# A fused transformer layer on one core: a rearranged start, a third PSUM bank for the maxima, and five small jobs moved between engines

## The chip, the cores and the metric

The kernel runs on one core of a Trainium2 chip. The metric is device time in microseconds (us) of one execution; lower is better. A core has a matrix engine (TensorE, PE; its weight loads are listed apart as PEld), a vector engine (VectorE, DVE), a scalar engine (ScalarE, ACT), a general engine (GpSimd, POOL), and queues that issue DMA transfers (here SP's and ACT's). PE writes its results into PSUM, which this kernel uses as eight banks of 128 partitions × 512 fp32 elements; all else lies in SBUF.

## The reference

One layer of a diffusion backbone. 128 context tokens (the prompt) and 1024 latent tokens are normalised and modulated, projected once, put through two groups of attention heads in parallel, gated, projected back, and added to the input.

```python
shift, scale, gate = modulation(c, w_mod[l], b_mod[l])          # silu(c) @ w_mod + b_mod
h = rmsnorm(xs, norm_gain[l]) * (1.0 + scale) + shift
q_a, k_a, v_a, g_a, q_b, k_b, v_b, g_b = project(h, w_in[l], ...)   # h @ w_in, RMS norm of q and k per head
...                                                             # rotary positions on q and k of latent tokens
o_a = global_attn_latent(q_a, k_a, v_a, cache_k_a[:, l], cache_v_a[:, l])            # all keys
o_b = window_attn_latent(q_b, k_b, v_b, cache_k_b[:, l], cache_v_b[:, l], sink_b[l])  # |i-j| <= 128, and a sink
xs = xs + gate * merge_out(o_a, g_a, o_b, g_b, w_out[l])        # concat(o_a*silu(g_a), o_b*silu(g_b)) @ w_out
```

The prompt goes through the same with its own modulation and sees only itself. D is 1024; each group has 8 query heads and 2 key heads of 64. Keys, values and the prompt's keys and values are outputs too.

## The kernel before

**Arithmetic.** Where fp32 accuracy is wanted, an operand is split into a high part in the matrix engine's fp32r type and the remainder, also fp32r: `hi` is a cast, `lo = raw - hi` a subtraction. A product is then three matmuls: hi·hi, hi·lo and lo·hi.

**Order.** The instructions of every engine run in the order in which the Python code emits them (`in_order` chains them). A small agenda puts work off: `later(n, f)` runs `f` at the n-th next `tick()`, and in attention one tick is one slot. So moving a line or changing a slot number moves instructions on every engine that it touches.

**The start.** Tokens come in nine tiles of 128 (tile 0 is the prompt, 1 to 8 are latent). `load_x` loads a tile through SP's queue; `squares` (ACT) and two small GpSimd operations give the reciprocal root mean square; `scaled` (DVE) multiplies; `turned_tile` transposes the tile on PE, by a 128×128 identity, into two PSUM tiles px (`px{t}_0` for the first four column blocks, `px{t}_1` for the others); `keep` copies them to `xT`. The identity comes by DMA (L321) and is cast to bf16 as `ident_b`. `modulate_rows(j)` (L353) multiplies the conditioning vectors with channel block j of the modulation weights `wm` (eight row products into one bank, pm, then one copy, mrows); `modulate(j)` transposes that back and reduces it to per-channel factors `a_mod`, `b_col`. `modulated(j, ...)` makes the block's input: ACT writes h's high part, DVE the full value hf, GpSimd the remainder (L410 to L412). `warm(n)` runs n matmuls of the bf16 identity with itself, whose result nobody reads (L431). The first gate product (L270) waits for `modulated(0, 1, 4, 0)`.

**The gates of mixer A.** A loop over channel blocks j = 1 to 8 adds channel block j-1's contribution to the gate columns: `first_gates` for the first 512 tokens, in banks `pg*_f`, and `next_gates` for the next 256 tokens, one block behind, in two banks `pg*_s`. After that come the queries, keys and values, the gates of mixer B, and the splits of the output weights w_out (16 pieces of 128×512; hi by a cast, lo by a subtraction, L1043 and L1044).

**Attention.** From about 298 us on the work runs in slots, one block of 128 keys against 512 queries (4 heads × 128) per slot. In each slot `scores` issues the score products (st, L1170 and L1171) or, for windowed heads, transposes of probabilities (L1165); ACT takes the exponential (pe, L1173) and its high part (ph, L1177), GpSimd or DVE the remainder (pl). Three slots later `values` multiplies with the value blocks (pv, L1191 to L1194). Between them the slot's due items run: row maxima for a later unit (pmx on PE, L889, then a maximum on DVE, L890), windowed scores in natural layout (sn, L944 and L945, DVE's mask and minimum L948, ACT's exponential pen, L934), transposes of small vectors, late pieces of w_out (`WO_LATE` gives the slot at which each is loaded; the split follows three slots later), and output products. At a unit's end, `inverse` (rs, L1203 for windowed heads, L1205 and L1206 for global ones), `gated` and `parts` (ogh, L1227, and its remainder) make the gated output's two parts.

**PSUM.** The eight banks carry letters: A, B, C with two each, D and E with one. In attention A serves pmx, sn and the small transposes in turn, B the scores, C the pv, D and E the two column halves of the output products (po); D also serves the last piece of mixer B's gates during the first slots.

A unit is one latent tile, one key head and one mixer: 9 slots for a global unit, 3 or 4 for a windowed one. Units 0 to 3 are latent tile 1 (24 slots), units 4 to 7 latent tile 2 (26 slots). Units 0 and 2 have their maxima taken before attention starts.

Of the kernel before, what the change touches and what calls it, by code (L numbers as in the profile page):

```python
# [50 lines left out]
WO_LATE = {12: 13, 13: 20, 11: 27, 14: 29, 15: 31}  # L51
# [10 lines left out]
LAST_ORDER = ((0, 0), (0, 1), (1, 0), (1, 1), (2, 0), (2, 1))  # L62
SECOND_FROM = 5
WARM = (8, 4)
# [51 lines left out]
def hybrid_step(ctx, tc, x_prompt, x_sample, cache_k_a, cache_v_a, cache_k_b, cache_v_b,  # L116
                cols, w_mod_ss, w_mod_g, b_mod, w_in, qn_a, kn_a, qn_b, kn_b, sink_b, w_out,
                k_ident, k_cos, k_sin, k_mask,
# [200 lines left out]
    with tc.tile_pool(name="st", bufs=2, side="right") as st:  # L319
        ident = st.tile([P, P], F32, name="ident", bufs=1)  # L320
        nc.sync.dma_start(ident, k_ident)  # L321
# [4 lines left out]
        nc.sync.dma_start(colt, cols)  # L326
# [22 lines left out]
        def modulate_rows(j):  # L349
            pm = pmod[j] = bank_tr(f"pm{j}")  # L350
            for k in range(KT):
                a = 32 * (k % 4)
                nc.tensor.matmul(pm[a : a + 32, 0:256], sil32[:, k, :], wm[j][:, k].rearrange("p s n -> p (s n)"),  # L353
                                 start=(k < 4), stop=(k >= 4), tile_position=(0, a))
            mrows[j] = st.tile([P, 256], F32, tag="mrows", name=f"mrows{j}")
            (nc.scalar.copy if j > 1 else nc.vector.tensor_copy)(mrows[j], pm[:, 0:256])
# [29 lines left out]
        def scaled(t):  # L386
            nc.vector.tensor_scalar(xn[t], xn[t], rx.pop(t), None, op0=ALU.mult)

        def turned_tile(t, tags, between=None):

            for c in range(2):
                if c and between:
                    between()
                px[t, c] = bank(tags[c], f"px{t}_{c}")
                for i in range(4):
                    k = 4 * c + i
                    nc.tensor.transpose(px[t, c][:, P * i : P * i + P], xn[t][:, P * k : P * k + P], ident)
# [5 lines left out]
        def modulated(j, t0, n, cond):  # L403

            w = P * n
            dst = slice(P * place(t0), P * place(t0) + w)
            i, to = third(dst)
            a, b = (x[:, j, cond : cond + 1] for x in (a_mod, b_col))
            hf = st.tile([P, 512], F32, tag="hf", name=f"hf{j}_{t0}", bufs=3)
            nc.scalar.activation(h_at(0, i, j, to), xT[:, j, dst], AF.Identity, scale=a, bias=b)  # L410
            nc.vector.tensor_scalar(hf[:, :w], xT[:, j, dst], a, b, op0=ALU.mult, op1=ALU.add)
            nc.gpsimd.tensor_tensor(h_at(1, i, j, to), hf[:, :w], h_at(0, i, j, to), op=ALU.subtract)  # L412
# [50 lines left out]
        modulated(0, 1, 4, 0)
# [5 lines left out]
        warm(WARM[1])  # L469
# [4 lines left out]
        for j in range(1, KT + 2):  # L474
# [397 lines left out]
    def max_items(i):  # L872
# [4 lines left out]
        def item(h, b):  # L877
# [4 lines left out]
            pm = bank("A", f"pmx{i}_{h}_{b}")  # L882
# [33 lines left out]
    def weight_items(i):  # L916
# [20 lines left out]
        def item(h):  # L937
# [5 lines left out]
            s = bank("A", f"sn{i}_{h}")[:, 0:n]  # L943
# [95 lines left out]
    def split_wo(i):  # L1039
        raw = wo_raw.pop(i)  # L1040
        hi, lo = (wo_place(j, i) for j in range(2))
        wo_parts[i] = hi, lo
        (nc.scalar.copy if i < 7 or i in WO_LATE else nc.vector.tensor_copy)(hi, raw)  # L1043
        (nc.gpsimd if i in WO_LATE or i % 2 else nc.vector).tensor_tensor(lo, raw, hi, op=ALU.subtract)  # L1044

# [111 lines left out]
    def scores(i, b, blk):  # L1157
# [4 lines left out]
        if m == 1:  # L1162
# [3 lines left out]
            nc.scalar.copy(ph, s)  # L1166
# [17 lines left out]
    def values(i, b, last, blk, ph, pl):  # L1184
# [15 lines left out]
        def inverse():  # L1200
            v["rs"] = w2.tile([64, 512], F32, tag="rs", name=f"rs{i}", bufs=1)
            if m == 1:
                nc.scalar.copy(v["rs"], pv[64:128, :])  # L1203
                return
# [16 lines left out]
        def parts():  # L1221
# [5 lines left out]
            nc.scalar.copy(oh, v["of"])  # L1227
# [90 lines left out]
    for s in range(len(slots) + LAG + PROMPT_END[3]):  # L1318
        tick()
# [29 lines left out]
def _consts():  # L1349
# [15 lines left out]
        "k_ident": np.eye(P, dtype=f),  # L1365
# [43 lines left out]
```

## Time and profile before

| | us |
|---|---|
| Time, median of 3 runs | 704.11 (703.66 to 704.31) |
| The profiled execution, its own time | 703.62 |
| Its span, first to last instruction | 701.4 |
| PE busy | 690.6 |
| DVE, ACT, POOL busy | 462.5, 419.2, 337.9 |
| First gate product starts | 16.76 |
| Attention slots start | about 298 |

A row of the timeline reads: start in us, duration in us, engine, line and operation, output <- inputs, partitions × elements and types, and in brackets how long the engine stood before it and on what. Several like instructions in a row are folded to one row with their count. PE's records overlap, so two starts are compared rather than a start with an end. The records name the line of the kernel that ran; in the changed kernel the same code has higher line numbers.

### The profile page before, as it was taken

To read this page: it belongs to the slowest core of one execution; us is meant where nothing else is said; L and a number is where in the kernel's file an instruction comes from. 1 tells how busy PE (TensorE), PEld (TensorE's weight loads), DVE (VectorE), ACT (ScalarE), POOL (GpSimd) and SP (SyncE) were. 2 spreads that over 40 slices of the span, in tenths; PEclk is the share of its full clock that TensorE was granted. 3 is DMA by queue.
4 is the path that set the end of the run, shared out by engine and by line. 5 is a ranking of instruction groups with operands and counts; after the bars stand their busy time and mean duration, and the time that the engine had idled before them with its cause. 6 is when DMAs were issued, how large, how long until landed. Compare 5 with 4: busy or idle time off the path is not lost.

```text
span 701.4 us, 10680 instructions
## 1 busy us (share of the span) xinstructions
PE 690.6 (98%) x3532; PEld 559.5 (80%) x3532; DVE 462.5 (66%) x998; ACT 419.2 (60%) x858; POOL 337.9 (48%) x358
## 2 busy tenths in 40 slices
PE   7999999999999999999999999999999999999997
PEld 4778988878788889986788787788887888887876
DVE  4667257968768854676667567567676775775563
ACT  6646411422313423399877887787788778877870
POOL 3547024233313321267676654765575557455752
PEclk9999999999999999999999999999999999999999
DMA  8962283349344016332222121122221221212324
GB/s 319 412 214 111 78 306 75 91 131 279 87 124 132 16 61 209 129 84 77 75 83 89 47 83 54 62 67 75 69 75 40 68 91 46 82 54 91 92 75 128
DMA packets 53703, 78.57 MB, mean 112 GB/s; under 512 B 7112, under 2 KB 25864, under 8 KB 52752
## 3 DMA queue, kind: packets, MB, share of 16 engines
q1 hardware_dynamic: 45952, 66.74, 28.9%
q10 hardware_dynamic: 7696, 11.15, 5.8%
q8 instruction: 28, 0.46, 0.3%
q14 instruction: 27, 0.22, 0.1%
HBM read 58.69 MB, written 19.18 MB: 111 GB/s over the span
## 4 chain that ended last, share of the span: by engine, by line
PE 94%; ACT 2%; DVE 2%; DMA 1%; issue 0%; POOL 0%; SPq 0%; ACTq 0%; DVEq 0%
PE po L1262 14%; PE pv L1191 7%; PE pv L1194 7%; PE pmx L889 5%; PE st L1170 5%; PE pv L1193 5%; PE pq L256 5%; PE pq L258 5%; PE st L1171 5%; PE pq L257 5%; PE st L1165 4%; PE pg L266 3%; PE pg L270 3%; PE pg L271 3%; PE pk L257 2%; PE pk L258 2%
## 5 line engine op out<-in xcount | busy, mean ns | idle before, releaser
L1181 POOL TENSOR_TENSOR pl<-pe,ph 128x512 fp32r<-128x512 f32 x130 | 167.8, 1293 | 142.7 <-DVE nm L948 64.4
L890 DVE TENSOR_REDUCE mx<-pmx 128x1 f32<-128x384 f32 x192 | 101.3, 552 | 58.5 <-PE pmx L889 56.0
L1173 ACT ACTIVATE pe<-st 128x512 f32<-128x512 f32 x146 | 86.8, 595 | 27.3 <-PE st L1171 26.5
L1177 ACT CAST ph<-pe 128x512 fp32r<-128x512 f32 x146 | 90.7, 621 | 4.8
L1191 PE MATMUL pv<-ph,v_hi 128*128 128x512 f32 x208 | 82.4, 396 | 0.1
L1194 PE MATMUL pv<-pl,v_hi 128*128 128x512 f32 x208 | 81.9, 394 | 0.0
L948 DVE CUSTOM_DVE_ANT_0 sn<-sn,mask,nsink 128x512 f32<-128x512 f32 (+1 forms) x64 | 46.3, 724 | 43.3 <-PE sn L945 39.2
L1262 PE MATMUL po<-wo,ogh 128*128 128x512 f32 (+1 forms) x224 | 73.2, 387 | 0.0
L181 POOL TENSOR_TENSOR rs_q<-ms_q,mhalf 128x8 f32<-128x8 f32 x18 | 34.1, 1896 | 80.9 <-DVE ms_q L179 80.9
L889 PE MATMUL pmx<-kha,qt 128*128 128x384 f32 x192 | 61.6, 365 | 1.1 <-ACT pen L934 0.8
L1170 PE MATMUL st<-qt,kha 128*128 128x512 f32 x144 | 57.7, 401 | 0.1
L1193 PE MATMUL pv<-ph,v_lo 128*64 128x512 f32 x146 | 57.7, 395 | 0.0
L1171 PE MATMUL st<-qb,kla 68*128 68x512 f32 x144 | 57.3, 398 | 0.0
L1194 PEld LDWEIGHTS pv<-pl,v_hi 128*128 128x128 f32 x208 | 39.0, 188 | 16.8
L934 ACT ACTIVATE pen<-sn,nm 128x512 f32<-128x512 f32 (+2 forms) x72 | 45.0, 626 | 5.7 <-DVE nm L948 2.3
L1166 ACT CAST ph<-st 128x512 fp32r<-128x512 f32 x62 | 36.4, 587 | 19.9 <-PE st L1165 19.6
L653 ACT CAST qo0q<-ptq 128x512 fp32r<-128x512 f32 x18 | 10.6, 586 | 60.4 <-PE ptq L650 58.8
L1262 PEld LDWEIGHTS po<-wo,ogh 128*128 128x128 f32 x224 | 41.0, 188 | 6.4
L1191 PEld LDWEIGHTS pv<-ph,v_hi 128*128 128x128 f32 x208 | 39.2, 189 | 7.8 <-issue 0.8
L1167 DVE TENSOR_TENSOR pl<-st,ph 128x512 fp32r<-128x512 f32 x62 | 42.6, 688 | 2.1 <-ACT ph L1166 1.4
L1262 PE MATMUL po<-wo,ogl 128*128 128x512 f32 (+1 forms) x112 | 43.5, 388 | 0.0
L889 PEld LDWEIGHTS pmx<-kha,qt 128*128 128x128 f32 x192 | 35.5, 190 | 7.3 <-DVE mx L890 1.8
(224 smaller groups left out, 1703.5 us busy)
## 6 DMA issues: line engine op xcount, KB each, us to landing
qt<-qd SPq DMA_DIRECT2D x36, 256.0 KB, 2.9
wm<-in_w_mod_ss_dram SPq DMA_DIRECT2D x7, 1024.0 KB, 9.7
qd<-qo0q ACTq DMA_DIRECT2D x36, 128.0 KB, 2.4
sgl<-gd SPq DMA_DIRECT2D x36, 128.0 KB, 2.3
out_dram<-yt SPq DMA_DIRECT2D x17, 256.0 KB, 2.1
xn<-in_x_sample_dram SPq DMA_DIRECT2D x8, 512.0 KB, 6.8
wg<-in_w_mod_g_dram SPq DMA_DIRECT2D x4, 1024.0 KB, 8.5
wraw<-in_w_out_dram SPq DMA_DIRECT2D x16, 256.0 KB, 4.5
```

The lines of the kernel that those rows point to most:

```text
L257: nc.tensor.matmul(out, h_at(0, i, k, tok), w.lo[k], start=False, stop=False)
L889: nc.tensor.matmul(pm[:, 0:384], lhs, kha[:, g, 3 * b : 3 * b + 3, :], start=True, stop=True)
L890: nc.vector.tensor_reduce(mx[:, h, b : b + 1], pm[:, 0:384], axis=AX.X, op=ALU.max)
L1170: nc.tensor.matmul(s, kh, qtile[i], start=True, stop=False)
L1171: nc.tensor.matmul(s, kl, qbtile[i], start=False, stop=True)
L1173: nc.scalar.activation(pe, s, AF.Exp)
L1177: nc.scalar.copy(ph, pe)
L1181: nc.gpsimd.tensor_tensor(pl, pe, ph, op=ALU.subtract)
L1191: nc.tensor.matmul(pv, two, ph, start=(b == 0), stop=False)
L1193: nc.tensor.matmul(pv[0:64, :], vl, ph, start=False, stop=False)
L1194: nc.tensor.matmul(pv, two, pl, start=False, stop=last)
L1262: nc.tensor.matmul(po[c][:, at], a, wo_parts[KT * n + k][lo][:, at], start=(k == KS[0] and p == 0), stop=(k == KS[-1] and p == 2))
```

## The change

- The identity is built on GpSimd (a fill and a select along the diagonal) instead of loaded; `colt`, the small table of columns, is loaded by ACT's queue. SP's first DMA is now x's.
- `modulate_rows(0)`, px3 and px4 are done in halves, with the halves that `modulate(0)` does not need behind it; `scaled(4)` is two instructions. `warm` runs 14 products first, then 2, 2 and 2 between the tiles, and 4 at the end, in place of 8 and 4.
- In `modulated(0, 1, 4, 0)` ACT writes h's first 256 columns and DVE the other 256.
- At j = 8 the small products of the first two column groups (six matmuls of 256 columns) go ahead of `first_gates` for channel block 7.
- pmx, sn and the two small transposes take banks A, A and E in turn until slot 24; after it A alone, as before.
- rs of unit 1 (a copy) goes from ACT to DVE, ogh of unit 0 from ACT to GpSimd. `PHB_DVE` is empty and changes nothing.
- The remainders of w_out 0, 2, 4, 6 go from DVE to GpSimd. The late pieces 12 and 13 are loaded at slots 23 and 24 instead of 13 and 20, pieces 11, 14 and 15 one slot earlier than before.

```diff
-WO_LATE = {12: 13, 13: 20, 11: 27, 14: 29, 15: 31}
+SMALL_FIRST = 2
+LO_POOL = (0, 2, 4, 6)
+WO_LATE = {12: 23, 13: 24, 11: 26, 14: 28, 15: 30}
...
+RS_DVE = (1,)
+PHB_DVE = ()
+OG_POOL = (0,)
+AUX = ((24, "AAE"),)
-WARM = (8, 4)
+WARM = (14, 2, 2, 2, 4)
...
+    aux_tags = ["A"]
+
+    def bank_aux(name):
+        turn["aux"] += 1
+        return bank(aux_tags[0][turn["aux"] % len(aux_tags[0])], name)
...
-        nc.sync.dma_start(ident, k_ident)
+        nc.gpsimd.memset(ident, 0.0)
+        nc.gpsimd.affine_select(ident, ident, pattern=[[-1, P]], compare_op=ALU.not_equal, fill=1.0, base=0,
+                                channel_multiplier=1)
...
-        nc.sync.dma_start(colt, cols)
+        nc.scalar.dma_start(colt, cols)
...
-        def modulate_rows(j):
-            pm = pmod[j] = bank_tr(f"pm{j}")
-            for k in range(KT):
+        def modulate_rows(j, ks=range(KT)):
+            if 0 in ks:
+                pmod[j] = bank_tr(f"pm{j}")
+            pm = pmod[j]
+            for k in ks:
...
+            if KT - 1 not in ks:
+                return
...
-            nc.scalar.activation(h_at(0, i, j, to), xT[:, j, dst], AF.Identity, scale=a, bias=b)
+            own = w // 2 if shared else w
+            nc.scalar.activation(h_at(0, i, j, slice(to.start, to.start + own)), xT[:, j, dst.start : dst.start + own],
+                                 AF.Identity, scale=a, bias=b)
+            if shared:
+                nc.vector.tensor_scalar(h_at(0, i, j, slice(to.start + own, to.stop)), xT[:, j, dst.start + own : dst.stop],
+                                        a, b, op0=ALU.mult, op1=ALU.add)
...
         warm(WARM[0])
-        for t, tags in ((1, "AB"), (2, "AB"), (3, "CC")):
+        for t in (1, 2):
             scaled(t)
-            turned_tile(t, tags)
+            turned_tile(t, "AB")
+            warm(WARM[t])
             if t > 1:
                 for c in range(2):
                     keep(t - 1, c, copies[c])
-        scaled(4)
-        modulate_rows(0)
+        scaled(3)
+        modulate_rows(0, range(4))
+        turned_half(3, 0, "C")
+        warm(WARM[3])
+        for c in range(2):
+            keep(2, c, copies[c])
+        scaled(4, 2)
+        modulate_rows(0, range(4, KT))
         keep(3, 0, copies[0])
         W_GA.split(nc.gpsimd)
-        turned_tile(4, "AB", lambda: modulate(0))
+        turned_half(4, 0, "A")
+        modulate(0)
         keep(4, 0, copies[0])
-        modulated(0, 1, 4, 0)
+        turned_half(3, 1, "C")
+        turned_half(4, 1, "B")
+        modulated(0, 1, 4, 0, True)
...
-        warm(WARM[1])
+        warm(WARM[4])
...
+            if j == KT:
+                for ch in range(SMALL_FIRST):
+                    next_gates(ch, j - 2)
             if big_on:
                 first_gates(0, j - 1, 0)
...
-                if small_on:
+                if small_on and not (j == KT and ch < SMALL_FIRST):
                     next_gates(ch, j - 2)
...
-            pm = bank("A", f"pmx{i}_{h}_{b}")
+            pm = bank_aux(f"pmx{i}_{h}_{b}")
...
-            s = bank("A", f"sn{i}_{h}")[:, 0:n]
+            s = bank_aux(f"sn{i}_{h}")[:, 0:n]
...
-        (nc.gpsimd if i in WO_LATE or i % 2 else nc.vector).tensor_tensor(lo, raw, hi, op=ALU.subtract)
+        (nc.gpsimd if i in WO_LATE or i % 2 or i in LO_POOL else nc.vector).tensor_tensor(lo, raw, hi, op=ALU.subtract)
...
-                nc.scalar.copy(v["rs"], pv[64:128, :])
+                (nc.vector.tensor_copy if i in RS_DVE else nc.scalar.copy)(v["rs"], pv[64:128, :])
...
-            nc.scalar.copy(oh, v["of"])
+            (nc.gpsimd.tensor_copy if i in OG_POOL else nc.scalar.copy)(oh, v["of"])
...
     for s in range(len(slots) + LAG + PROMPT_END[3]):
+        aux_tags[0] = next((tags for until, tags in AUX if s < until), "A")
```

What moves where, at three places. PE's program between the transposes of tile 3 and the first gate product, before (x4 marks four like instructions; xn_181 is tile 3, xn_183 tile 4):

```order
L397 MATMUL px_0_268<-ident,xn_181 128x128 x4
L397 MATMUL px_1_273<-ident,xn_181 128x128 x4
L353 MATMUL pm_281<-wm_185,sil_173 32x256 x8
L397 MATMUL px_0_299<-ident,xn_183 128x128 x4
L362 MATMUL pm_281<-ident,mrows_290 128x128 x2
L397 MATMUL px_1_310<-ident,xn_183 128x128 x4
```

The same stretch now (xn_184 is tile 3, xn_186 tile 4):

```order
L369 MATMUL pm_283<-wm_188,sil_176 32x256 x4
L414 MATMUL px_0_288<-ident,xn_184 128x128 x4
L457 LDWEIGHTS ident_b
L457 MATMUL idle<-ident_b 128x512
L457 LDWEIGHTS ident_b
L457 MATMUL idle<-ident_b 128x512
L369 MATMUL pm_283<-wm_188,sil_176 32x256 x4
L414 MATMUL px_0_313<-ident,xn_186 128x128 x4
L380 MATMUL pm_283<-ident,mrows_304 128x128 x2
L414 MATMUL px_1_325<-ident,xn_184 128x128 x4
L414 MATMUL px_1_330<-ident,xn_186 128x128 x4
```

Both second halves (px_1) now stand behind the transposes of the modulation rows.

PE's program at j = 8, before: the products of h's remainder (h_0_7_130, L266) come as the fifth and sixth step.

```order
L270 MATMUL pg_0_f<-h_0_7_122,whiga_789 128x512
L271 MATMUL pg_0_f<-h_0_7_122,wloga_790 128x512
L270 MATMUL pg_1_f<-h_0_7_122,whiga_789 128x512
L271 MATMUL pg_1_f<-h_0_7_122,wloga_790 128x512
L266 MATMUL pg_0_f<-h_0_7_130,whiga_789 128x512
L266 MATMUL pg_1_f<-h_0_7_130,whiga_789 128x512
```

The same place now:

```order
L282 MATMUL pg_0_s<-h_1_6_134,whiga_738 128x256
L283 MATMUL pg_0_s<-h_1_6_134,wloga_739 128x256
L278 MATMUL pg_0_s<-h_1_6_138,whiga_738 128x256
L282 MATMUL pg_0_s<-h_1_6_134,whiga_738 128x256
L283 MATMUL pg_0_s<-h_1_6_134,wloga_739 128x256
L278 MATMUL pg_0_s<-h_1_6_138,whiga_738 128x256
L282 MATMUL pg_0_f<-h_0_7_122,whiga_809 128x512
L283 MATMUL pg_0_f<-h_0_7_122,wloga_810 128x512
L282 MATMUL pg_1_f<-h_0_7_122,whiga_809 128x512
L283 MATMUL pg_1_f<-h_0_7_122,wloga_810 128x512
L278 MATMUL pg_0_f<-h_0_7_130,whiga_809 128x512
```

Six products of the other 256 tokens stand ahead.

ACT's program in latent tile 1, from the exponential of the third windowed score of unit 1 on, before:

```order
L934 ACTIVATE pen_3609,sum_3611<-sn_2_3651,nm_3610 128x384
L1203 COPY rs_3662<-pv_3618 64x512
L1173 ACTIVATE pe_3_3669<-st_3_3664 128x512
L1177 CAST ph_3_3665<-pe_3_3669 128x512
L1043 CAST wo_big_3683<-wraw_3633 128x512
L934 ACTIVATE pen_3609,sum_3611<-sn_3_3673,nm_3610 128x384
L1173 ACTIVATE pe_4_3693<-st_4_3688 128x512
L1177 CAST ph_4_3689<-pe_4_3693 128x512
L1227 CAST ogh_3703<-spare 128x256
```

Now:

```order
L973 ACTIVATE pen_3629,sum_3631<-sn_2_3669,nm_3630 128x384
L1212 ACTIVATE pe_3_3687<-st_3_3682 128x512
L1216 CAST ph_3_3683<-pe_3_3687 128x512
L973 ACTIVATE pen_3629,sum_3631<-sn_3_3691,nm_3630 128x384
L1212 ACTIVATE pe_4_3707<-st_4_3702 128x512
L1216 CAST ph_4_3703<-pe_4_3707 128x512
```

Between the exponentials stood a copy (rs), a cast of w_out (wo_big) and a cast of the gated output (ogh); all three are gone from ACT here.

More of the change, by code (lines that the diff above doesn't have):

```diff
@@ L117, in hybrid_step @@
                 cols, w_mod_ss, w_mod_g, b_mod, w_in, qn_a, kn_a, qn_b, kn_b, sink_b, w_out,
-                k_ident, k_cos, k_sin, k_mask,
+                k_cos, k_sin, k_mask,
                 y_prompt, y_sample, new_k_a, new_v_a, new_k_b, new_v_b):
@@ L146, in hybrid_step @@
     BANKS = {"A": 2, "B": 2, "C": 2, "D": 1, "E": 1}
-    turn = {"mm": 0, "tr": 0}
+    turn = {"mm": 0, "tr": 0, "aux": 0}
     mm_tags = ["BAAB"]
@@ L384, in squares, with scaled, turned_half, turned_tile @@
             nc.gpsimd.tensor_tensor(rx[t], ms, mhalf[:, 0:1], op=ALU.pow)
-        def scaled(t):
-            nc.vector.tensor_scalar(xn[t], xn[t], rx.pop(t), None, op0=ALU.mult)
-        def turned_tile(t, tags, between=None):
-            for c in range(2):
[L392 to L397, printed above, removed]
+        def scaled(t, parts=1):
+            r = rx.pop(t)
+            for p in range(parts):
+                half = xn[t][:, D // parts * p : D // parts * (p + 1)]
+                nc.vector.tensor_scalar(half, half, r, None, op0=ALU.mult)
+        def turned_half(t, c, tag):
+            px[t, c] = bank(tag, f"px{t}_{c}")
+            for i in range(4):
+                k = 4 * c + i
+                nc.tensor.transpose(px[t, c][:, P * i : P * i + P], xn[t][:, P * k : P * k + P], ident)
+        def turned_tile(t, tags):
+            for c in range(2):
+                turned_half(t, c, tags[c])
         def keep(t, c, copy):
@@ L401, in keep, with modulated @@
             copy(xT[:, 4 * c : 4 * c + 4, at], px.pop((t, c)).rearrange("p (k n) -> p k n", n=P))
-        def modulated(j, t0, n, cond):
+        def modulated(j, t0, n, cond, shared=False):
             w = P * n
@@ L904, in transpose @@
         def transpose():
-            pt = bank("A", f"ptm{i}")
+            pt = bank_aux(f"ptm{i}")
             nc.tensor.transpose(pt[0:4, 0:P].bitcast(F32R), m_nat[i // 2 % 2], ident_r)
@@ L994, in turned @@
         def turned():
-            v["pt"] = bank("A", f"pti{i}")[0:4, 0:P]
+            v["pt"] = bank_aux(f"pti{i}")[0:4, 0:P]
             nc.tensor.transpose(v["pt"], v["inv"], ident_r.bitcast(F32))
@@ L1165, in scores @@
                 nc.tensor.transpose(s[:, P * h : P * h + P], penat[i][:, h, o : o + P], ident_r.bitcast(F32))
-            nc.scalar.copy(ph, s)
+            (nc.vector.tensor_copy if (i, b) in PHB_DVE else nc.scalar.copy)(ph, s)
             later(1, lambda: nc.vector.tensor_tensor(pl, s, ph, op=ALU.subtract))
@@ L1364, in _consts @@
     return {
-        "k_ident": np.eye(P, dtype=f),
         "k_cos": lay(np.cos(ang)),
```

## The prediction

> **What bounds the kernel now.** I read the page first (span, busy time, the chain that ended last), then the waits of TensorE, then the timeline wherever a wait had its place. From the page:
>
> ```profile
> span 701.4 us, 10680 instructions
> PE 690.6 (98%) x3532; PEld 559.5 (80%) x3532; DVE 462.5 (66%) x998; ACT 419.2 (60%) x858; POOL 337.9 (48%) x358
> PE 94%; ACT 2%; DVE 2%; DMA 1%; issue 0%; POOL 0%; SPq 0%; ACTq 0%; DVEq 0%
> ```
>
> TensorE (PE) is busy for 98% of the span and is 94% of the chain of waits. A change that leaves its products as they are, as this one does but for 12 more dummy products at the start, can win only the time in which PE stands or is slowed. The waits of PE (total us, times, longest) name the places:
>
> ```profile
> PE idle L431 <- DVE ident_b L323: 3.4, 1, 3.4
> PE px L397 <- DVE xn L387: 1.2, 1, 1.2
> PE pmx L889 <- ACT pen L934: 0.8, 1, 0.8
> PE pg_f L270 <- ACT h L410: 0.4, 1, 0.4
> PE sn L944 <- ACT pen L934: 0.4, 2, 0.2
> PE pmx L889 <- DVE mx L890: 0.2, 1, 0.2
> PE pg_f L266 <- POOL h L412: 0.2, 1, 0.2
> ```
>
> They are 6.6 us, at three places: the start, one product near 61 us (L266), and attention in latent tile 1 (L889, L944). Waits hide part of the loss, because a product that was late also shows a longer record. So I compare starts: undisturbed products of 512 columns start 0.232 us apart, those of 384 columns 0.174 us:
>
> ```profile
> 60.09 0.40 PE L270 MATMUL pg_f<-h,whiga 128*128 128x512 f32 x1
> 60.32 0.40 PE L271 MATMUL pg_f<-h,wloga 128*128 128x512 f32 x1
> 316.80 0.34 PE L944 MATMUL sn<-khb,qt 128*128 128x384 f32 x1
> 316.97 0.33 PE L945 MATMUL sn<-klb,qt 128*128 128x384 f32 x1
> ```
>
> Set against these, the loss is 16.76 us ahead of the first gate product, 0.33 at 60.9, and 3.9 in 316 to 333 us (worked out below). The profiled execution took 703.62 us, 2.2 more than its span, and lies 0.49 under the median of the runs; the sum is made for it, and 0.49 added at the end.
>
> **Part 1, the start.** What counts is when the first gate product starts; everything behind it moves along.
>
> ```profile
> 0.72 0.40 SPq L321 DMA_DIRECT2D ident<-in_k_ident_dram  x1
> 1.64 1.85 SPq L375 DMA_DIRECT2D xn<-in_x_sample_dram  x4
> 3.38 3.60 PE L431 MATMUL idle<-ident_b 128*128 128x512 bf16 x8 [3.38 <-DVE ident_b L323]
> 3.53 1.00 SPq L334 DMA_DIRECT2D wm<-in_w_mod_ss_dram  x2
> 8.16 3.27 PEld L397 LDWEIGHTS px<-ident,xn 128*128 128x128 f32 x16 [2.09 <-DVE xn L387]
> 9.05 1.06 ACT L380 ACTIVATE sq<-xn 128x1024 bf16<-128x1024 f32 x1 [1.27 <-DMA xn<-in_x_sample_dram]
> 11.95 0.86 PEld L397 LDWEIGHTS px<-ident,xn 128*128 128x128 f32 x8 [0.51 <-DVE xn L387]
> 12.61 0.76 DVE L387 TENSOR_SCALAR xn<-xn,rsx 128x1024 f32<-128x1024 f32 x1
> 12.97 1.07 PE L353 MATMUL pm<-wm,sil 128*32 128x256 f32 x16
> 15.89 0.81 ACT L410 ACTIVATE h<-xT,b_col,a_mod 128x512 fp32r<-128x512 f32 x1 [0.64 <-DVE b_col L368]
> 16.76 0.50 PE L270 MATMUL pg_f<-h,whiga 128*128 128x512 f32 x1 [0.43 <-ACT h L410]
> wm<-in_w_mod_ss_dram SPq DMA_DIRECT2D x2, 512.0 KB, 8.0
> ```
>
> SP's queue loses ident and colt, so the x loads issue at 0.72 instead of 1.64: 0.92 earlier, and so does wm. Squares of tile 3 wait for a DMA (9.05), so squares 3 and 4 and the scaling of tile 4 (12.61) follow: 11.69, its halves done near 12.1 and 12.45. Wm's two parts (issued 0.5 apart, 8.0 to land) are there at about 10.6 and 11.1. Then PE runs the first half of the modulation rows, px3's first half, two dummy products, the second half of the rows (0.53, half of 1.07), px4's first half (4 at 0.108): done at about 12.95. The copy of the rows runs beside px4. Before, from the end of the row products (12.97 + 1.07 = 14.04) to h (15.89) went 1.85, for the copy, two transposes, a reduction, a_mod and b_col; now the row products end near 12.5, which gives h at about 14.4. H itself is halved between ACT and DVE: 0.4 to 0.5 instead of 0.87 to the product. First gate product: about 15.0 to 15.3, gain 1.45 to 1.75. Against it stand PE's own queue, and the clock. 14 dummies at 0.45 (3.60 / 8, the slow pace) take 6 us. The identity is now made on GpSimd, by an operation the trace lacks. If that costs 0.3 to 0.6 us (nearest rows below), the dummies begin near 2.2 and end at 8.2, where px1 could have started at 7.25. Weight loads of the transposes took 0.204 each from 8.16 (3.27 / 16) and 0.108 from 11.95: the clock doubled in that run. If it rises only at 9.0, PE reaches the first gate product at about 15.9, gain 0.8. I take 1.2, between the two; the bounds are 0 (identity a further microsecond late) and 2.0.
>
> [...]
>
> **Part 2, the small products ahead at channel block 8.** The products of the remainder h (L266) waited for GpSimd:
>
> ```profile
> 59.42 0.28 PE L266 MATMUL pg_s<-h,whiga 128*128 128x256 f32 x1
> 59.53 0.48 PE L270 MATMUL pg_f<-h,whiga 128*128 128x512 f32 x1
> 60.88 0.73 PE L266 MATMUL pg_f<-h,whiga 128*128 128x512 f32 x2 [0.16 <-POOL h L412]
> ```
>
> From 60.32 to 60.88 is 0.56 for a step of 0.23: 0.33 lost. Six products of 256 columns, 0.12 apart, go ahead: 0.7 us of work, over twice the wait. Gain 0.33; with the late step at 59.53 0.42; if GpSimd is itself later, 0.
>
> **Part 3, latent tile 1.** PE, PEld, DVE, ACT, POOL in the window, each with its count:
>
> ```profile
> 316.32:332.75 16.43, 14.90 (x60) 9.80 (x60) 10.04 (x24) 15.55 (x33) 12.20 (x13) 1.00 0.24 75
> ```
>
> 58 steps, 42 of 512 and 16 of 384 columns, would take 42 × 0.232 + 16 × 0.174 = 12.53; they took 16.43, so 3.9 is lost. ACT is busy for 15.55 of the 16.43: here ACT is the bound, and PE waits for its exponentials. Three ACT operations go elsewhere:
>
> ```profile
> 323.13 0.58 ACT L1203 COPY rs<-pv 64x512 f32<-64x512 f32 x1
> 323.74 0.60 ACT L1173 ACTIVATE pe<-st 128x512 f32<-128x512 f32 x1
> 324.90 0.61 ACT L1043 CAST wo_big<-wraw 128x512 fp32r<-128x512 f32 x1
> 325.42 0.57 ACT L934 ACTIVATE pen<-sn,nm 128x384 f32<-128x384 f32 x1
> 327.13 0.40 ACT L1227 CAST ogh<-spare 128x256 fp32r<-128x256 f32 x1
> 327.43 0.59 ACT L1173 ACTIVATE pe<-st 128x512 f32<-128x512 f32 x1
> ```
>
> From each to the next: rs 0.61 (now DVE's), w_out 12 0.52 (now tile 2's), ogh 0.30 (now GpSimd's): 1.43 off ACT, and off PE as far as PE waits for it. The third bank for pmx and sn lets PE issue them before ACT or DVE has read the one but last: the 0.8 at L889 and 0.2 at L944 are waits for a bank. Walked step by step with ACT's operations closed up, these waits remain: 0.73 for exponentials of the scores two slots earlier, 0.49 for the last pen, 0.4 for DVE's maxima, 1.62 in all. Gain 3.9 - 1.6 = 2.3. Least: 1.0, if the DVE copy and GpSimd's cast are late themselves (GpSimd is busy 12.20 of 16.43); most: all 3.9. The 0.58 on DVE (busy 10.04) and 0.40 on GpSimd are covered by those idle 6.4 and 4.2 us; without that cover they come back as waits of 0.6 and 0.4.
>
> **Part 4, latent tile 2 and the early remainders.** The casts of w_out 12 and 13 (0.52 each) and their remainders now fall here:
>
> ```profile
> 338.00:362.00 24.00, 24.00 (x118) 19.35 (x116) 14.30 (x32) 20.23 (x42) 17.71 (x18) 1.00 0.27 86
> L1044 POOL TENSOR_TENSOR wo_big<-wraw,wo_big 128x512 fp32r<-128x512 f32 x4 | 5.2, 1288 | 0.0
> ```
>
> PE stood nowhere here; ACT has 3.8 us to spare, GpSimd 6.3. Two casts (1.0) and two remainders (2.6) fit on the whole; a single exponential arrives up to 1.0 later where PE is 0.4 to 1.25 ahead of needing it. Cost 0.1, from 0 to 0.8. The four early remainders on GpSimd (1.29 instead of DVE's 0.71) lie where PE works on gates and maxima without a wait: nothing, at most 0.2.
>
> **Sum.** 703.62 - 1.2 - 0.33 - 2.3 + 0.1 = 699.9; with 0.49, 700.4. I put 700.3.
>
> **The rivals.**
> B, new waits take the old ones' place: ACT stays the bound of tile 1 (15.55 - 1.43 = 14.1 of work for 12.5 of PE), the clock rises late. Start 0.8, block 8 0.33, tile 1 1.0, tile 2 -0.5: 1.6 gained, 702.5. For it speaks ACT's sum; against it that exponentials may run ahead with PE closer up.
> C, every wait goes: 2.0 + 0.42 + 3.9 = 6.3, 697.8. Against it: ACT's 14.1.
> D, the change doesn't do what it says: a slow identity eats the start, GpSimd and ACT give the rest back: within 0.2% of before, 703.6.
> E, slower: the identity. GpSimd's price for an unknown operation lies between these rows:
>
> ```profile
> L181 POOL TENSOR_TENSOR rs_q<-ms_q,mhalf 128x8 f32<-128x8 f32 x18 | 34.1, 1896 | 80.9 <-DVE ms_q L179 80.9
> L733 POOL TENSOR_SCALAR v_hi<-gain 128x256 fp32r<-128x256 f32 x5 | 2.0, 402 | 0.0
> ```
>
> At 237 ns a column (1896 / 8, a power) 128 columns take 30 us, and the dummies begin near 32 instead of 2.2; with the 13.7 of the slow-clock case (15.9 - 2.2) the first gate product starts near 45.5, 28.7 later than before, and with the other gains of 2.5 the time is about 730. At 1.6 ns a column (402 / 256) it takes 0.2, and with the cost of issue 0.3 to 0.6. A select and fill is nearer to the second. Beyond an identity at about 2 us each microsecond costs one; the gains of 3.7 are eaten, and the kernel is slower than before, from about 6.
>
> **How the numbers follow.** A 0.60, B 0.22, C 0.06, D 0.08, E 0.04. A measurement tells about 0.2% here, 1.4 us. B's lower half lies within that of before: 0.05 of its 0.22. Faster 0.60 + 0.17 + 0.06 = 0.83; same 0.08 + 0.05 = 0.13; slower 0.04. A's own range, from its terms' halfway bounds, is 699.2 to 701.6; B and half of C widen it to 698.3 to 703.0, with D's upper part and E outside.
>
> **What would show it.** The first gate product at 15 to 16 us (this part right), at 16.5 or later (wrong), and the identity's own rows on GpSimd: under 1 us or not. At block 8 no wait at L266's successor. In 316 to 333 the same 58 steps in about 14.1 us instead of 16.43, ACT without rs, w_out and one ogh, and no wait of pmx for pen of 0.8. In 338 to 362 PE's steps stay undisturbed; a wait of PE for ACT or POOL there refutes part 4. If the gap between the runs and 700.3 is all in tile 1, the hand walk was wrong; if all in the start, the clock or the identity.

## The result, and the profile after

The changed kernel takes 699.75 us (median of 6 runs, 699.49 to 700.10) against 704.15 (6 runs, 703.66 to 704.31). The ratio is 0.9938, 95% interval 0.9926 to 0.9951: 0.6% faster. The forecast was 700.3 with a range of 698.3 to 703.0. The profiled execution took 699.49 with a span of 697.7. The page of the changed kernel, and its waits of TensorE (total us, times, longest):

```profile
span 697.7 us, 10706 instructions
PE 690.8 (99%) x3544; PEld 559.3 (80%) x3544; DVE 461.3 (66%) x997; ACT 418.7 (60%) x856; POOL 344.2 (49%) x365
```

```profile
PE idle L457 <- DVE ident_b L337: 2.0, 1, 2.0
PE pmx L928 <- ACT pen L973: 0.3, 1, 0.3
PE st L1209 <- ACT pe L1212: 0.2, 1, 0.2
```

Of 6.6 us of waits 2.5 are left. To see where the time went I matched each product of PE with the same product in the trace of before, and subtracted the starts. "Lead" below is by how many us a product comes earlier than before; a stage's gain is the lead behind it less the lead ahead of it.

| stage | forecast | measured | lead behind it |
|---|---|---|---|
| start, to the first gate product | 1.2 | 1.80 | 1.80 |
| channel block 1's row products | - | -0.20 | 1.60 |
| channel block 8 | 0.33 | 0.53 | 2.13 |
| maxima beside the w_out splits, 276 us | 0 | 0.27 | 2.39 |
| latent tile 1 | 2.3 | 1.60 | 3.99 |
| latent tile 2 | -0.1 | -0.24 | 3.75 |
| the rest of the span | 0 | -0.02 | 3.73 |

The start, from the timeline of the changed kernel:

```profile
0.73 1.82 SPq L393 DMA_DIRECT2D xn<-in_x_sample_dram  x4
1.00 0.29 POOL L334 TENSOR_SCALAR_AFFINE_SELECT ident<-ident 128x128 f32<-128x128 f32 x1
2.03 5.69 PE L457 MATMUL idle<-ident_b 128*128 128x512 bf16 x14 [2.03 <-DVE ident_b L337]
7.34 1.01 PEld L414 LDWEIGHTS px<-ident,xn 128*128 128x128 f32 x8
10.92 0.88 DVE L408 TENSOR_SCALAR xn<-xn,rsx 128x512 f32<-128x512 f32 x2
11.85 0.64 PE L369 MATMUL pm<-wm,sil 128*32 128x256 f32 x8
14.96 0.49 PE L282 MATMUL pg_f<-h,whiga 128*128 128x512 f32 x1
15.75 0.40 PE L283 MATMUL pg_f<-h,wloga 128*128 128x512 f32 x1
16.29 1.07 PE L369 MATMUL pm<-wm,sil 128*32 128x256 f32 x16
```

The select took 0.29 us, the identity was there at 1.3, and the transposes of tile 1 already run at the fast pace (8 weight loads take 1.01, where 16 took 3.27 before; the products start 0.11 apart, from 7.56 to 8.32). From 15.75 to the row products at 16.29 go 0.54 instead of 0.33 (17.56 to 17.89 before): this is the 0.20 that is given back.

Channel block 8 runs without a gap, and the products of the remainder follow at 59.58:

```profile
58.53 0.28 PE L278 MATMUL pg_s<-h,whiga 128*128 128x256 f32 x1
58.65 0.40 PE L282 MATMUL pg_f<-h,whiga 128*128 128x512 f32 x1
59.35 0.40 PE L283 MATMUL pg_f<-h,wloga 128*128 128x512 f32 x1
59.58 0.62 PE L278 MATMUL pg_f<-h,whiga 128*128 128x512 f32 x2
```

Latent tile 1 and 2 in windows (PE, PEld, DVE, ACT, POOL busy, each with its count, then the granted clock and two figures of the DMA), and PE's late products in tile 1:

```profile
313.92:328.75 14.83, 14.18 (x60) 9.90 (x60) 10.25 (x24) 13.88 (x30) 10.72 (x13) 1.00 0.19 57
338.00:362.00 24.00, 24.00 (x116) 18.99 (x115) 14.94 (x31) 20.46 (x43) 20.58 (x20) 1.00 0.31 99
```

```profile
318.10 0.50 PE L1209 MATMUL st<-qt,kha 128*128 128x512 f32 x1 [0.18 <-ACT pe L1212]
318.44 0.40 PE L1210 MATMUL st<-qb,kla 68*128 68x512 f32 x1
322.75 0.45 PE L928 MATMUL pmx<-kha,qt 128*128 128x384 f32 x1 [0.31 <-ACT pen L973]
326.94 1.27 PE L928 MATMUL pmx<-kha,qt 128*128 128x384 f32 x3
```

The same 58 steps take 14.83 instead of 16.43, of which 12.53 is undisturbed work: 2.30 is still lost. In tile 2 GpSimd is busy 20.58 of 24 instead of 17.71, and without a break from 338.2 to 357.4. There PE waits once, for the remainder that it multiplies with (pl, L1220), which stands behind one of w_out on GpSimd:

```profile
351.73 1.30 POOL L1083 TENSOR_TENSOR wo_big<-wraw,wo_big 128x512 fp32r<-128x512 f32 x1
352.96 2.55 POOL L1220 TENSOR_TENSOR pl<-pe,ph 128x512 fp32r<-128x512 f32 x2
354.32 0.51 PE L1233 MATMUL pv<-pl,v_hi 128*128 128x512 f32 x1
```

### The profile page after: what moved, and what is told of

Its sections match the earlier page's. It is cut to its first block, busy times and chain, and to the rows that moved or that the text cites. A ratio compares the mean times of both kernels' runs of the same rounds, so it can differ in the third digit from the quotient of the medians.

```text
span 697.7 us, 10706 instructions
## 1 busy us (share of the span) xinstructions
PE 690.8 (99%) x3544; PEld 559.3 (80%) x3544; DVE 461.3 (66%) x997; ACT 418.7 (60%) x856; POOL 344.2 (49%) x365
## 4 chain that ended last, share of the span: by engine, by line
PE 97%; DMA 1%; ACT 1%; DVE 0%; issue 0%; POOL 0%; SPq 0%; POOLq 0%; ACTq 0%
PE po L1301 14%; PE pv L1230 7%; PE pv L1233 7%; PE pmx L928 5%; PE st L1209 5%; PE pv L1232 5%; PE st L1210 5%; PE pq L268 5%; PE pq L270 5%; PE pq L269 5%; PE st L1204 4%; PE pg L278 3%; PE pg L282 3%; PE pg L283 3%; PE pk L269 2%; PE pk L270 2%
## 5 line engine op out<-in xcount | busy, mean ns | idle before, releaser
L1220 POOL TENSOR_TENSOR pl<-pe,ph 128x512 fp32r<-128x512 f32 x130 | 168.1, 1295 | 140.5 <-DVE nm L987 64.1
```

Of the source, the lines that this page charges most:

```text
L1220: nc.gpsimd.tensor_tensor(pl, pe, ph, op=ALU.subtract)
```

## The experiments

All are edits of the changed kernel, but for the fourth. The ratio is to the kernel before, run beside it; 699.75 is the changed kernel's median.

| edit | time, us | ratio, 95% | first gate product | tile 1 stage |
|---|---|---|---|---|
| (changed kernel) | 699.75 | 0.9938 (0.9926 to 0.9951) | 14.96 | 14.83 |
| identity by DMA | 700.52 | 0.9954 (0.9939 to 0.9969) | 16.17 | 14.55 |
| 8 dummies | 700.26 | 0.9948 (0.9933 to 0.9963) | 15.80 | 14.80 |
| h whole on ACT | 700.08 | 0.9947 (0.9932 to 0.9962) | 15.55 | 14.81 |
| before, identity on GpSimd | 703.29 | 0.9994 (0.9985 to 1.0004) | 15.73 | 16.67 |
| no small products first, remainders on DVE | 700.53 | 0.9949 (0.9931 to 0.9967) | 15.24 | 14.81 |
| two banks | 700.22 | 0.9944 (0.9929 to 0.9960) | 15.14 | 15.45 |
| rs, ogh, w_out 12 and 13 back | 701.06 | 0.9961 (0.9947 to 0.9975) | 15.12 | 16.96 |
| w_out 12 and 13 back | 700.54 | 0.9949 (0.9931 to 0.9967) | 15.12 | 16.05 |
| four banks | 700.05 | 0.9944 (0.9929 to 0.9959) | 15.61 | 14.38 |
| remainder of w_out 14 on DVE | 700.66 | 0.9953 (0.9936 to 0.9970) | 15.14 | 14.80 |
| weights of block 1 first | 699.61 | 0.9938 (0.9923 to 0.9952) | 15.34 | 14.81 |
| four banks, DVE's order, weights first | 698.99 | 0.9926 (0.9912 to 0.9939) | 14.99 | 14.13 |

Six of these kernels have the changed kernel's start word for word (no small products first, two banks, both that bring work back to tile 1, four banks, w_out 14). Their first gate product comes between 15.12 and 15.61, so that 14.96 is an early one: the start's gain is 1.15 to 1.80, by when the x tiles land. (In all seven traces it follows the first squares of x, which start when their tile has landed, at 4.38 to 5.14, by 10.46 to 10.58.) In these six the row products of block 1 follow the product ahead by 0.32 or 0.33, so that with this order of loads the 0.20 is lost only after so early a first product. The tile 1 stage scatters too: where its code is the changed kernel's, six further traces give 14.55 and 14.80 to 14.81, and where it is the code of before, 16.43 and 16.67. The kernel before, run beside the experiments, had medians of 703.73 to 704.12. Whole times of single edits are read with this in mind; stages are read from leads within one trace.

**Identity by DMA.**

```diff
-        nc.gpsimd.memset(ident, 0.0); nc.gpsimd.affine_select(ident, ident, ...)
-        nc.scalar.dma_start(colt, cols)
+        nc.sync.dma_start(ident, k_ident)
+        nc.sync.dma_start(colt, cols)
```

> The changed kernel, with the identity and the column table loaded by SP's queue again. Theory (the x loads set the start, and each place in SP's queue costs 0.46): the x loads issue at 1.64 instead of 0.73, 0.91 later, and the first gate product starts at 15.9 (14.96 + 0.91); total about 700.6 against the changed kernel's 699.75. Rival (PE's own program paces the start, from the identity on): the dummies begin at 3.38 instead of 2.03, and the first gate product comes 1.35 later, at 16.3. Second rival (the order in halves carries the gain by itself): no later than 15.2.

```profile
3.42 5.51 PE L455 MATMUL idle<-ident_b 128*128 128x512 bf16 x14 [3.42 <-DVE bsc L352]
8.77 1.04 PE L412 MATMUL px<-ident,xn 128*128 128x128 f32 x8
16.17 0.50 PE L282 MATMUL pg_f<-h,whiga 128*128 128x512 f32 x1
```

16.17 lies between theory (15.9) and rival (16.3): the 14 dummies begin 1.4 later and push the first transposes from 7.56 to 8.77, later than the x loads alone would. Of the lead 0.59 is left at the first gate product. The order in halves does not carry the gain by itself.

**8 dummies.**

```diff
-WARM = (14, 2, 2, 2, 4)
+WARM = (8, 0, 0, 0, 4)
```

> The changed kernel with 8 dummy products at the start instead of 14 and none between the tiles (4 at the end stay). In the changed kernel the pace of the dummies went from 0.43 to 0.21 at 7.13 us, ahead of the first transpose. Theory (the added dummies raise the clock early, and that is part of the gain): the transposes of tiles 1 and 2 run at 0.21 each again, PE is late for the halves of tile 3, and the first gate product starts at 15.3 to 15.9; total up to 0.9 above the changed kernel. Rival (the loads of x and of the modulation weights pace the start, the dummies are idle work): 14.96 within 0.1, total unchanged.

```profile
7.55 3.27 PEld L414 LDWEIGHTS px<-ident,xn 128*128 128x128 f32 x16 [2.84 <-DVE xn L408]
11.75 0.42 PEld L414 LDWEIGHTS px<-ident,xn 128*128 128x128 f32 x4 [0.41 <-issue]
15.80 0.50 PE L282 MATMUL pg_f<-h,whiga 128*128 128x512 f32 x1
```

The theory held in this execution: transposes at 0.204 again (3.27 / 16), first gate product 15.80. The dummies are worth up to 0.8, and 0.7 against the kernels whose first squares began alike (15.12 to 15.14). But the four runs spread from 699.25, under all six of the changed kernel, to 700.71, more than those of any other edit of the changed kernel; their mean clocks are 0.999 in the two shorter and 0.997 in the two longer. Where the lower mean clock comes from, no trace shows: the profiled run is one of the two shorter. Between the end of the dummies (5.6) and the row products at 11.16 only transposes ran, and behind them the pace was 0.105 (0.42 / 4 at 11.75). In the kernel before it was so too: dummies to 6.98, then transposes alone to 12.97, the first sixteen at 0.204 and the last eight at 0.108.

**H whole on ACT.**

```diff
-        modulated(0, 1, 4, 0, True)
+        modulated(0, 1, 4, 0)
```

> The changed kernel with ACT writing all 512 columns of the first h. Theory: h is ready 0.27 later (0.87 instead of 0.60), the first gate product starts at 15.2; but the row products of channel block 1, which start at 16.29 and stood for their weights, start no later than 16.35, so that the total rises by less than 0.1. Rival (those row products follow the gate products, not their weights): the 0.25 stays to the end, total 0.25 above the changed kernel.

From the second half of the row products to the first gate product it took 3.26 (12.29 to 15.55), against 3.03 to 3.11 in the other kernels with halves and 14 dummies: sharing is worth some 0.2 there. Nothing of it was made good behind, so the mechanism that the theory named (block 1's weights as a floor) did not act, as h came late anyhow. The median is 0.33 above the changed kernel's, but the spans of the four runs (697.8 to 698.0) lie within the changed kernel's six (697.7 to 698.3); the difference lies outside the span, which the last part comes back to. Whether the 0.2 stays to the end is not settled.

**Before, with the identity on GpSimd.**

```diff
 (kernel before)
-        nc.sync.dma_start(ident, k_ident)
-        nc.sync.dma_start(colt, cols)
+        nc.gpsimd.memset(ident, 0.0); nc.gpsimd.affine_select(ident, ident, ...)
+        nc.scalar.dma_start(colt, cols)
```

> The kernel before, with nothing but the identity built on GpSimd and the column table on ACT's queue. Theory (queue order): x loads 0.91 earlier, and the first gate product moves from 16.76 to 15.85; total 703.2 against 704.1. Rival (the clock stays slow through the transposes, or halves are needed to use the earlier x): 16.4 or later.

The first gate product moved to 15.73, 1.03 earlier, and the lead at the end of the trace is 1.01: the theory's 0.91 nearly. (In between it rose to 1.30 at 276 us, and fell to 1.06 in tile 1.) The 24 transposes of tiles 1 to 3 took 4.51, little less than the 4.88 before, and it mattered little here. In time the ten runs (702.53 to 704.16) don't tell it from before. So queue order brought 1.0 of the start, halves and dummies together 0.35 to 0.6 (the lead that is left when the identity comes by DMA).

**No small products first, remainders on DVE.**

```diff
-SMALL_FIRST = 2
-LO_POOL = (0, 2, 4, 6)
+SMALL_FIRST = 0
+LO_POOL = ()
```

> The changed kernel without two edits that lie 200 us apart: the six small products behind the large ones again at channel block 8, and the w_out remainders 0, 2, 4, 6 on DVE again. Theory: at 60 us PE loses 0.53 (a stall of 0.33, and the steps beside it 0.09 and 0.11 longer), at 276 us 0.27 (a product of maxima waits until DVE, held by a remainder, has read its bank); total 0.8 above the changed kernel. Rival: the 0.27 is not the remainder's doing, and only 0.53 comes back.

At block 8 the lead stands at 1.39 ahead and 1.38 behind: the 0.53 is gone, as expected. At 276 us it rises by 0.12, so 0.15 of the 0.27 went with the remainders. In every trace with these on GpSimd it rises by 0.25 to 0.27. In the kernel before with the identity alone, where these remainders are DVE's too, nothing was lost there at all (the lead rose by 0.26). The stall (DVE sits in the remainder while a bank waits for its maximum) comes with the remainders on DVE, but not in each execution: 0 to 0.27.

**Two banks.**

```diff
-AUX = ((24, "AAE"),)
+AUX = ()
```

> The changed kernel with bank A alone for maxima and windowed scores. The step from unit 1's first score product to the windowed scores of unit 3 took 14.83 us in the changed kernel and 16.43 before. Theory (ACT's three operations were the larger part, the bank the smaller): 15.3 to 15.5, total 0.5 to 0.7 above the changed kernel. Rival (the bank is what matters, ACT's work only moves): 16.0 or more, total 1.2 or more above.

The stage takes 15.45, as expected: beside the moved jobs the third bank is worth 0.62, and without it they bring 0.98. The total is 0.47 above the changed kernel's, a little under the theory's 0.5 to 0.7.

**Rs, ogh and w_out 12 and 13 back.**

```diff
-WO_LATE = {12: 23, 13: 24, 11: 26, 14: 28, 15: 30}
-RS_DVE = (1,)
-OG_POOL = (0,)
+WO_LATE = {12: 13, 13: 20, 11: 26, 14: 28, 15: 30}
+RS_DVE = ()
+OG_POOL = ()
```

> The changed kernel with the copy rs, the cast ogh and the splits of w_out 12 and 13 back at their old places (bank E stays). Theory (ACT bounds this stage): 14.83 becomes 16.0 to 16.2 for the stage, and tile 2 no longer loses its 0.25, so the total is 0.9 to 1.1 above the changed kernel. Rival (the bank alone does it): the stage stays under 15.2, and the total falls by up to 0.2.

The stage took 16.96, more than before the change, and for a reason that neither theory had. Windows of this kernel; the column behind POOL's is the granted clock:

```profile
321.60:325.00 3.40, 1.72 (x8) 1.10 (x8) 0.00 (x0) 3.31 (x8) 3.40 (x5) 1.00 0.10 29
325.00:328.40 3.40, 3.40 (x10) 2.53 (x9) 2.67 (x5) 2.97 (x7) 2.90 (x4) 0.51 0.28 89
```

```profile
322.51 0.50 PE L1209 MATMUL st<-qt,kha 128*128 128x512 f32 x1 [0.84 <-ACT pe L1212]
324.25 0.45 PE L928 MATMUL pmx<-kha,qt 128*128 128x384 f32 x1 [0.83 <-ACT pen L973]
326.22 0.63 PE L1230 MATMUL pv<-ph,v_hi 128*128 128x512 f32 x1
326.65 0.63 PE L1232 MATMUL pv<-ph,v_lo 128*64 128x512 f32 x1
```

After two waits of 0.84 and 0.83 within 3.4 us the granted clock was 0.51 for 3.4 us (325.0 to 328.4; 1.00 ahead of it, 0.99 behind it); products came 0.43 apart instead of 0.23. Two of the five runs show a mean clock of 0.997 to 0.998 (701.71 and 701.91, the profiled one among them), the other three 0.999 to 1.000 (700.84 to 701.06). Those three are 1.1 to 1.3 above the changed kernel in time; their spans (698.7 to 698.9) are 0.75 to 0.95 above its median span of 697.95, about the theory's 0.9 to 1.1, and the rest lies outside the span. So the bank alone does not do it. Which of the jobs brought back costs this, the next experiment shows.

**W_out 12 and 13 back.**

```diff
-WO_LATE = {12: 23, 13: 24, 11: 26, 14: 28, 15: 30}
+WO_LATE = {12: 13, 13: 20, 11: 26, 14: 28, 15: 30}
```

> The changed kernel with only the splits of w_out 12 and 13 back in latent tile 1 (loads at slots 13 and 20). Theory: ACT gets 0.52 of work back in the stage, PE loses 0.4 to 0.5 there and wins 0.25 in tile 2, where GpSimd was busy without a break; total 0.2 above the changed kernel. Rival: the stage has slack for the cast now, and moving the splits cost more than it brought: total 0.25 below.

The stage takes 16.05: not 0.4 to 0.5 but 1.22 is lost for one cast of 0.52 (w_out 12's; that of 13, at 332.59, lies behind the stage). Tile 2 loses nothing, as expected. The spans (698.6 to 698.8) are only some 0.1 under those of the three runs above, so that beside w_out 12 the copy rs and the cast ogh, 0.91 of ACT's work, seem to cost next to nothing; what they cost without it was not tried. ACT's sum of work alone does not set the price. The other 0.7 is on DVE. Its remainder of block 4 (pl, L1218), here, in the changed kernel, and with four banks, each beside GpSimd's operation at that time. With w_out 12 back:

```profile
324.39 1.29 POOL L1083 TENSOR_TENSOR wo_big<-wraw,wo_big 128x512 fp32r<-128x512 f32 x1
...
324.50 1.73 DVE L1218 TENSOR_TENSOR pl<-pe,ph 128x512 fp32r<-128x512 f32 x1 [3.14 <-POOL pl L1220]
326.15 1.01 DVE L929 TENSOR_REDUCE mx<-pmx 128x1 f32<-128x384 f32 x2
...
326.75 0.44 PE L928 MATMUL pmx<-kha,qt 128*128 128x384 f32 x1 [0.48 <-DVE mx L929]
```

The changed kernel:

```profile
323.13 1.30 POOL L1220 TENSOR_TENSOR pl<-pe,ph 128x512 fp32r<-128x512 f32 x1
...
323.94 1.03 DVE L1218 TENSOR_TENSOR pl<-pe,ph 128x512 fp32r<-128x512 f32 x1 [2.62 <-ACT ph L1216]
```

With w_out 12 back it began 1.18 before GpSimd's operation ended and took 1.73; in the changed kernel 0.49 before and 1.03; 0.69 is its median (16 in the changed kernel). In both it ended some 0.55 after GpSimd's. So w_out 12 costs its cast on ACT, and on DVE the time by which the remainder beside GpSimd's is longer (1.73 instead of 0.69); behind that the maxima wait, whose banks PE waits for (0.48 at 326.75). Why DVE's operation is longer there, no trace shows.

**Four banks.**

```diff
-AUX = ((24, "AAE"),)
+AUX = ((9, "AAE"), (24, "AAED"))
```

> The changed kernel with bank D as a fourth in the turn from slot 9 to slot 24. Theory: in 313.9 to 328.75 the waits of pmx for pen (0.31) and for DVE's maxima (0.48 in slot 20) are waits for a bank and go; those of the scores for ACT (0.62) stay; total 0.5 to 0.8 under the changed kernel. Rival: DVE is what is late, its maxima queue behind the remainder of block 4, and PE loses the same time a little later: less than 0.2.

The rival's outcome held, its mechanism did not. The stage fell to 14.38, by 0.45, and right behind it 0.37 was lost again, not to DVE but to GpSimd, which had three remainders in a row. The total is 0.30 above the changed kernel's: in the trace the first gate product came late (15.61), and in all four runs 2.2 lies outside the span. The rows at the loss:

```profile
325.87 1.29 POOL L1220 TENSOR_TENSOR pl<-pe,ph 128x512 fp32r<-128x512 f32 x1
327.27 0.74 POOL L1256 TENSOR_TENSOR spare<-spare,sgl 128x256 f32<-128x256 f32 x1
...
328.80 3.78 POOL L1220 TENSOR_TENSOR pl<-pe,ph 128x512 fp32r<-128x512 f32 x3
...
330.16 0.49 PE L1233 MATMUL pv<-pl,v_hi 128*128 128x512 f32 x1
```

**Remainder of w_out 14 on DVE.**

```diff
-(nc.gpsimd if i in WO_LATE or i % 2 or i in LO_POOL else nc.vector)
+(nc.gpsimd if i != 14 and (i in WO_LATE or i % 2 or i in LO_POOL) else nc.vector)
```

> The changed kernel with the remainder of w_out 14 on DVE (0.69) instead of GpSimd (1.30), in latent tile 2. Theory: the remainder of the probabilities comes 1.2 earlier from GpSimd, PE's one stall of tile 2 (0.25 at 354 us) goes, total 0.25 under the changed kernel. Rival: DVE is then late with its maxima, and nothing is won.

Worse than either: tile 2 loses 0.98 instead of 0.24. DVE stood 0.99 for ACT's cast and then took 1.13 for the remainder, and PE's maxima, which queue behind, were late:

```profile
349.25 1.13 DVE L1083 TENSOR_TENSOR wo_big<-wraw,wo_big 128x512 fp32r<-128x512 f32 x1 [0.99 <-ACT wo_big L1082]
...
350.90 0.91 PE L928 MATMUL pmx<-kha,qt 128*128 128x384 f32 x2 [0.45 <-DVE mx L929]
```

**Weights of block 1 first.**

```diff
-        load_x(5)
-        load_wm(1)
+        load_wm(1)
+        load_x(5)
```

> The changed kernel with the modulation weights of channel block 1 loaded ahead of x tile 5 in SP's queue, where they no longer stand behind a load that waits for its buffer until 8.63 us. Theory: the row products of channel block 1 wait for these weights; they start at 16.0 instead of 16.29, and 0.2 of the start's gain that was given back stays; total 0.2 under the changed kernel. Rival: the earlier transfer takes bandwidth from the weights of block 0 or the first gate weights, whose landing sets the second half of the row products (11.85), and the first gate product comes later by 0.3 or more.

The time, 699.61, is not told apart from the changed kernel's. Here the first gate product came late (15.34, though the first squares began as in the kernels with 15.12 to 15.14: the dummies ran longer, and the first transposes started at 7.97 instead of 7.57), and the weights would have been there in any case. The last kernel, whose first gate product came at 14.99, shows it: its row products start at 16.12, 0.32 after the product ahead, not 0.54. But some 0.1 is lost again at 27.3 us, where the changed kernel loses nothing, and ahead of block 8 the lead is 1.64 against 1.60: little of the 0.2 stays. No harm to the first block is seen there.

**Four banks, DVE's order, weights first.**

```diff
+AUX = ((9, "AAE"), (24, "AAED"))
...
-        if b in PL_DVE:
-            later(1, lambda: nc.vector.tensor_tensor(pl, pe, ph, op=ALU.subtract))
+        if b in PL_DVE or (i, b) == (2, 5):
+            later(2 if (i, b) == (2, 4) else 1, lambda: nc.vector.tensor_tensor(pl, pe, ph, op=ALU.subtract))
...
-        load_x(5)
-        load_wm(1)
+        load_wm(1)
+        load_x(5)
```

> The changed kernel with three edits: bank D as a fourth in the turn from slot 9 to 24; in unit 2 the remainder of block 4 stands on DVE behind the two maxima that it held up, and that of block 5 goes from GpSimd to DVE; and the weights of channel block 1 are loaded ahead of x tile 5. With four banks alone the stage took 14.38 instead of 14.83, but 0.37 of it was lost at 330 us, where PE waited for a remainder of GpSimd's, which had queued 1.3 behind block 5's. Theory (queue order on DVE and GpSimd is what is left to win here, beside ACT): the stage takes 14.0 to 14.4, nothing is lost at 330 us, total 699.2 (0.4 to 0.6 under the changed kernel). Rival (ACT, with 14.1 of work, bounds the stage whatever the others do): the stage stays at 14.3 or more, total 699.6 or above.

```profile
313.90:328.03 14.13, 13.81 (x59) 9.96 (x59) 10.55 (x24) 13.20 (x29) 10.13 (x12) 1.00 0.22 64
...
322.46 1.02 DVE L929 TENSOR_REDUCE mx<-pmx 128x1 f32<-128x384 f32 x2 [1.15 <-PE pmx L928]
...
324.26 1.64 DVE L1218 TENSOR_TENSOR pl<-pe,ph 128x512 fp32r<-128x512 f32 x2
...
326.80 0.70 PE L928 MATMUL pmx<-kha,qt 128*128 128x384 f32 x3
```

The theory held: 14.13 for the stage, nothing lost at 330 us. The two maxima run at 322.5 instead of 324.9, no maximum waits for a bank, and of what is left (1.6 over 12.53) 0.61 is two waits of the scores for ACT's exponentials (at 318.08 and 321.51); the rest are steps that come 0.07 to 0.20 late. The three edits were not taken apart. The time is 698.99; its five runs (698.82 to 699.36) all lie under the changed kernel's six. It is the fastest of all here: 0.74% under before.

## Why the prediction was right, and where its terms were off

The time was right to 0.08% (700.3 was put, where the terms add up to 700.4), and the four places of gain and loss were the ones named, but the sum was nearer than its terms: that their errors cancel is luck.

- **Start, 1.2 forecast, 1.80 then 1.60.** "If it rises only at 9.0, PE reaches the first gate product at about 15.9" was the step that failed: the pace rose within the dummies (14 in 5.69; their weight loads start 0.43 apart up to the one at 7.13, the load behind it 0.21 later), and the first of the two estimates (15.0 to 15.3) was the right one. What the prediction and the expectations call the clock there is PE's pace: the granted clock reads 1.00 on both sides of its rise (in the kernel before from 8.16 to 11.43, at 0.204 a transpose, and from 11.95 to 12.80, at 0.108), and no run shows a clock behind it. The x loads were worth 1.03 alone (0.92 forecast). The identity cost 0.5 on GpSimd (a fill of 0.20 and the select of 0.29), within 0.3 to 0.6; rival E fell with it. The wait of 0.20 for block 1's weights was not in the sum.
- **Channel block 8, 0.33 forecast, 0.53.** The stall was rightly sized. The steps ahead of it (59.53, 0.09, which the prediction gave as its 0.42 and left out of the sum) and after it (60.88, 0.11, not seen) were longer too, and went with it.
- **Tile 1, 2.3 forecast, 1.60.** "Walked step by step ... 1.62 in all" failed by 0.7 (by 0.4 in the shortest trace of the same stage, 14.55). The waits named were there: for the scores 0.62 (0.73 forecast), for pen 0.47 (0.49), for maxima 0.48 (0.4). Missing was that the product after a late one is itself 0.10 to 0.11 late: 318.10 to 318.44 is 0.34 where 0.23 is undisturbed. Five such steps are 0.54 (one of them, from 319.82, behind a product that was on time). The price of single jobs was off more widely: 0.52 for w_out 12 was 1.22, for beside its remainder on GpSimd DVE's took 1.73 instead of 0.69. For rs and ogh the covers named (DVE's and GpSimd's idle time) seem to have held: no wait of PE for either is in the trace.
- **Tile 2, -0.1 forecast, -0.24.** Within the bounds; the place was GpSimd's queue, not ACT's exponentials.
- **Early remainders, 0 forecast, up to 0.27 gained.** DVE's maxima there do sometimes wait behind a remainder; I had taken that part of the gates to run without a wait.
- **Outside the span, not forecast, 0.4 gained.** The changed kernel takes 1.8 us beyond its span, before 2.2. In the experiments it is 1.8 to 1.9 in some kernels and 2.1 to 2.2 in others (h whole, four banks, the identity alone, ACT's work back; w_out 14 with 2.0 to 2.2), steady from run to run of a kernel. No trace here shows what it is, and it stays open.

The errors of start, block 8, remainders and the time outside the span (0.4 + 0.2 + 0.27 + 0.4) and those of the tiles (-0.7 - 0.14) leave 0.4 in favour of the kernel. Rival B's mechanism (ACT stays the bound) was at work in tile 1 in part: 1.09 of the 2.30 that are left there are waits for its exponentials (0.62 and 0.47).

## What to carry to other kernels

Cost a job by the engines that it touches in turn, not by its own time: a cast of 0.5 us cost 1.2 here, since beside its second half on another engine an operation of a third took 1.73 instead of 0.69, behind which stood what freed a bank; beside it, 0.9 of other work on the same engine seemed to cost some 0.1. In a queue that runs in order, an operation that waits for another engine belongs behind those that free buffers; that, and a fourth bank, brought what the third bank had not (14.13 for the stage instead of 14.83). Where PE's stalls are counted, count the product after each too: here it came 0.10 to 0.11 late.

## What the runs showed of the hardware that was not expected

- With ACT's work back in tile 1, TensorE's granted clock fell in mid-kernel, and no wait in the 3.40 us ahead of it (321.6 to 325.0) was longer than 0.84. With 1.72 us of work there, in pieces, the granted clock was 0.51 for the next 3.40 (325.0 to 328.4); of the five runs this one and another have the lower mean clocks (0.998 and 0.997). What makes it fall, no trace shows. The kernel before shows no fall in a stretch with 2.49 of 3.41 busy, the clock again behind POOL's column, nor in the 3.39 behind it (1.00):

```profile
323.90:327.31 3.41, 2.49 (x10) 1.47 (x9) 0.32 (x1) 3.35 (x8) 3.41 (x5) 1.00 0.20 56
```

- DVE's remainder of the probabilities (pl, L1218) took 0.69 us (the median of 16 in the changed kernel), or 1.03 and 1.73 where it began 0.49 and 1.18 before the end of a GpSimd operation; it then ended some 0.55 after it.
- The same start gave a first gate product between 14.96 and 15.61 us, by the landing of the x tiles (first squares at 4.38 to 5.14).
